# The norm of the next block from columns of the prompt, in blocks 1 to 3 of layer 0

## The chip, the cores and the metric

The kernel runs on one core of a Trainium2 chip. The metric is the time of one execution in microseconds of the device: a median of 2242.0 us in 3 runs (2238.49 to 2245.57). On the core, TensorE (PE) does matmuls and transposes, VectorE (DVE), ScalarE (ACT) and GpSimd (POOL) work on elements, and SyncE (SP) issues nearly all transfers from one queue, in program order.

## The reference

The reference is one step of a decoder with two layers, on a prompt of 2048 tokens and a batch of eight single new tokens. The width is 1024. Each layer normalises its input, projects it to 3332 columns, lets four token mixers (retention, HGRN2, S5, Mamba-2) work on groups of these columns, gates and joins their outputs, projects back and adds the result to the stream. The change touches the norm alone:

```
def rms_norm(x, w):
    xf = x.astype(jnp.float32)
    y = xf * lax.rsqrt(jnp.mean(xf * xf, axis=-1, keepdims=True) + EPS)
    return (y * w.astype(jnp.float32)).astype(x.dtype)
```

Every token is divided by the root mean square of its row, and every column is multiplied by a weight. The projections are computed in float32 precision from pairs of rounded values: each operand is split into a high part (fp32r) and a low part, the rest, and three matmuls (low by high, high by low, high by high) add up to one product.

## The kernel before

The prompt is cut into four blocks of 512 tokens, and each layer goes through its four blocks, so that there are eight blocks in all. For each block the normalised input stands in eight tiles hn, one for every 128 columns, each 128 columns (partitions) by 512 tokens, with a high and a low half. The matmuls want columns on the partitions, while the stream lies in memory by rows, a token after the other. So the norm has to transpose.

The projection of a block is made in four parts, gemm_A, gemm_H, gemm_M and gemm_S. The norm of the next block runs during the last, gemm_S: norm_stats has read the rows of the next block before that and has their reciprocal root mean squares in a small tile xn_rs (128 tokens by 4). norm_block (L567 to L596) is a generator of five steps, called between the passes of the last four pairs of gemm_S (L633 is the matmul of these passes). Its steps are:

- fetch (L570 to L577) brings 256 columns of all 512 rows into one of two xn buffers (L572, 512 KB). ACT multiplies two of the four groups of rows by xn_rs (L575, two instructions), and DVE the other two (L577, one instruction).
- For each of the two groups of 128 columns in a fetch, PE transposes four squares of 128x128 into a PSUM bank (L589), ACT writes the high half of hn from that bank times the weight (L591), and DVE writes the low half as the bank times the weight less the high half (L592).
- The next fetch into the same buffer follows.

PE runs in the order of the program. The other engines and their queues are ordered by a scheduler, which puts ready instructions by priority: weights (L687 to L689, load, cast and rest; L615 and L616 for the other kind of projection) have the highest, token mixers (L912 to L925 for HGRN2, L1604 to L1653 for Mamba-2, where one step of 128 tokens has its transposes L1604 and L1605, the matmuls L1611 and L1615, and later L1632, L1636 and L1639) come behind. Of the rest of what the prediction names: L793 adds up the four parts of the projection of the eight single tokens from a PSUM bank; L1585 is a multiplication on POOL; L502 to L526 are the setup of the S5 tables, with transfers through scratch tables in memory (s5c, gpad); L534 is the reading of rows by norm_stats. PSUM banks of the token mixers and the transposes come from one pool of four (mb), which go round in the order of the program. SG below is the second half of gemm_S, and RV the projection of the next part that follows it, whose matmul is L695; its weights go through six buffers wr.

Of the kernel before, what the change touches and what calls it, by code (L numbers as in the profile page):

```python
# [11 lines left out]
F32 = mybir.dt.float32  # L12
F32R = mybir.dt.float32r
BF16 = mybir.dt.bfloat16
I32 = mybir.dt.int32
AF = mybir.ActivationFunctionType
ALU = mybir.AluOpType
# [4 lines left out]
P = 128  # L22
D = 1024
KT = 8
TB = 512
# [88 lines left out]
def trunk_kernel(ctx: ExitStack, tc: tile.TileContext, A: dict):  # L114
    nc = tc.nc
    V, G, S, T = nc.vector, nc.gpsimd, nc.scalar, nc.tensor
# [12 lines left out]
    hnp = pool("hn", NHN)  # L129
    wrp = pool("wraw", NWR)  # L130
    whp = pool("whl", NWH)
    xnp = pool("xn", NXN)
# [13 lines left out]
    def nm(s):  # L146
        uid[0] += 1
        return f"{s}_{uid[0]}"
# [6 lines left out]
    def half(shape=(P, 512), dt=F32):  # L155
        if alt[0] and AH[alt[0]]:
            return smp.tile(list(shape), dt, name=nm("half"), tag="half" + alt[0], bufs=AH[alt[0]])
        return halfp.tile(list(shape), dt, name=nm("half"), tag="half")
# [22 lines left out]
    def mbank():  # L181
        return mps.tile([P, 512], F32, name=nm("mb"), tag="mb")
# [7 lines left out]
    mats = ctile([P, M_W], "mats")  # L190
    x_first = [big() for _ in range(4)]
    nw_rows = half([P, P])[0:8]
    with tc.high_priority(offset=2000):
        nc.sync.dma_start(x_first[0], x_in[0:P, :])
        nc.sync.dma_start(mats[:, 0:P], A["c_mats"][:, 0:P])
        nc.sync.dma_start(nw_rows, A["norm_w"][0].rearrange("(a p) -> a p", p=P))
        nc.sync.dma_start(x_first[1], x_in[P : 2 * P, :])
# [4 lines left out]
    lvl = ctile([P, 127], "lvl", I32)  # L202
    nc.sync.dma_start(lvl, A["c_lvl"])
    ident = mats[:, M_ID : M_ID + P]
# [335 lines left out]
    def norm_first(hn):  # L540
        ps = mbank()
        T.transpose(ps[:, 0:8], nw_rows, mats[:8, M_ID : M_ID + 8])
        nw = small([P, 8], "nw_first", bufs=1)
        V.tensor_copy(nw, ps[:, 0:8])
        rss = []
        for tt, xt in enumerate(x_first):
            ss, rs = small([P, 1], "nf_ss", bufs=4), small([P, 1], "nf_rs", bufs=4)
            S.activation(half((P, 1024), BF16), xt, AF.Square, accum_out=ss)
            rsqrt(rs, ss, 1, 1.0 / D)
            rss.append(rs)  # L550
        for tt, xt in enumerate(x_first):
            tsl = slice(tt * P, (tt + 1) * P)
            rs = rss[tt]
            V.tensor_scalar(xt, xt, rs, None, ALU.mult)
            for k4 in range(2):
                ps = mbank()
                for i in range(4):
                    kt = 4 * k4 + i
                    T.transpose(ps[:, i * P : (i + 1) * P], xt[:, kt * P : (kt + 1) * P], ident)
                for i in range(4):  # L560
                    kt = 4 * k4 + i
                    pk = ps[:, i * P : (i + 1) * P]
                    S.activation(hn[kt][:, 0, tsl], pk, AF.Identity, scale=nw[:, kt : kt + 1])
                    V.scalar_tensor_tensor(hn[kt][:, 1, tsl], pk, nw[:, kt : kt + 1], hn[kt][:, 0, tsl].bitcast(F32), ALU.mult, ALU.subtract)
            yield 0

    def norm_block(L, rows, rs, hn):  # L567
        xts = {}
# [1318 lines left out]
    layers = []  # L1887
    for l in range(DEPTH):
        L = Layer()
# [58 lines left out]
    with tc.manual_schedule(engines={mybir.EngineType.PE}):  # L1948
# [19 lines left out]
        for i, B in enumerate(blocks):  # L1968
            nxt = blocks[i + 1] if i + 1 < nblk else None
# [24 lines left out]
            rows, rs = norm_stats(nxt.b, srcdst(nxt.l)[0])  # L1994
# [9 lines left out]
                drain(prep)  # L2004
            if nxt.l != B.l:
                drain(load)
            norm = norm_block(layers[nxt.l], rows, rs, nxt.hn)
            run(gemm_S(B.L, B), lambda n: next(norm, 0) if n >= 3 else None)
            for _ in norm:
                pass  # L2010
# [42 lines left out]
```

## Time and profile before

| | before |
|---|---|
| median of 3 runs | 2242.0 us (2238.49 to 2245.57) |
| the profiled execution | 2245.02 us |
| its span | 2243.2 us |
| mean granted clock of PE | 0.98 |
| PE busy | 2118.9 us, 94% |
| DVE busy | 1669.3 us, 74% |
| ACT busy | 1034.2 us, 46% |
| POOL busy | 239.5 us, 11% |
| bytes moved | 284.41 MB, mean 127 GB/s |

The span is the stretch of the profiled execution from its first to its last instruction. Busy shares are means over the whole; the work in one stretch is read from views of that stretch alone. An engine with a full share there sets how fast the others get on.

### The profile page before, as it was taken

How to read it: one execution, taken by the hardware profiler on the slowest of the kernel's cores; microseconds unless marked ns; L12 is line 12 of the kernel's file. 1: busy time of each engine (PE TensorE's matmuls, PEld its weight loads, DVE VectorE, ACT ScalarE, POOL GpSimd, SP SyncE). 2: the span in 40 equal slices, each digit the busy share in tenths (PEclk: the TensorE clock that was granted, in tenths of full speed). 3: DMA queues.
4: the chain of work that ended last, by engine and by line, in shares of the span. 5: the costliest groups of instructions: out<-in, count | busy, mean ns of one | idle time of the engine just before them, and what ended most of it. 6: DMA issues, size and time to landing. Idle time of an engine off the chain costs nothing. (4 is left out here: it accounts for less than half of the span.)

```text
span 2243.2 us, 41062 instructions
## 1 busy us (share of the span) xinstructions
PE 2118.9 (94%) x15031; PEld 1712.8 (76%) x15031; DVE 1669.3 (74%) x4614; ACT 1034.2 (46%) x1889; POOL 239.5 (11%) x212
## 2 busy tenths in 40 slices
PE   7999989999999999999999998999899899999996
PEld 7778767776777877788877876777677678878786
DVE  6888666898749977787747867489985687748774
ACT  7434433456333564346453453444634245454343
POOL 0112011000210002201100011000120001100100
PEclk9999999999999999999999999999999999999999
DMA  6324633236524364374533335334652253431272
GB/s 213 104 66 120 182 104 118 90 108 203 143 67 143 94 196 121 115 167 126 179 97 112 95 113 165 99 109 119 202 154 78 86 163 101 156 92 50 68 260 94
DMA packets 263354, 284.41 MB, mean 127 GB/s; under 512 B 88752, under 2 KB 183616, under 8 KB 263152
## 3 DMA queue, kind: packets, MB, share of 16 engines
q1 hardware_dynamic: 263152, 281.79, 42.4%
q8 instruction: 118, 1.93, 0.4%
q14 instruction: 84, 0.69, 0.1%
HBM read 245.52 MB, written 31.99 MB: 124 GB/s over the span
## 5 line engine op out<-in xcount | busy, mean ns | idle before, releaser
L695 PE MATMUL gb<-wh,hn 128*128 128x512 f32 x2208 | 542.1, 400 | 3.4 <-DVE half L1650 2.3
L633 PE MATMUL gb<-hn,wh 128*128 128x512 f32 x1920 | 485.9, 406 | 10.3 <-DVE wh L616 6.9
L695 PEld LDWEIGHTS gb<-wh,hn 128*128 128x128 f32 x2208 | 409.9, 188 | 109.1 <-issue 11.6
L633 PEld LDWEIGHTS gb<-hn,wh 128*128 128x128 f32 x1920 | 359.9, 192 | 99.2 <-DVE wh L616 8.1
L689 DVE TENSOR_TENSOR wh<-wr,wh 128x512 fp32r<-128x512 f32 x296 | 215.3, 732 | 242.6 <-ACT wh L688 239.2
L688 ACT CAST wh<-wr 128x512 fp32r<-128x512 f32 x296 | 183.2, 620 | 373.5 <-PE gb L695 193.6
L695 PE MATMUL gb<-wh,mx 128*128 128x512 f32 x1344 | 341.5, 407 | 7.9 <-DVE half L1733 5.8
L695 PEld LDWEIGHTS gb<-wh,mx 128*128 128x128 f32 x1344 | 251.3, 192 | 77.8 <-DVE half L1733 10.1
L615 ACT CAST wh<-wr 128x512 fp32r<-128x512 f32 (+1 forms) x248 | 152.3, 619 | 308.4 <-PE gb L633 83.5
L616 DVE TENSOR_TENSOR wh<-wr,wh 128x512 fp32r<-128x512 f32 (+1 forms) x248 | 183.3, 745 | 77.6 <-ACT wh L615 74.2
L628 PE MATMUL gb<-wh,hn 128*128 128x256 f32 (+1 forms) x1728 | 220.2, 286 | 11.1 <-DVE convc L1524 4.7
L628 PEld LDWEIGHTS gb<-wh,hn 128*128 128x128 f32 x1728 | 211.6, 191 | 15.8 <-issue 9.2
L1585 POOL TENSOR_TENSOR half<-mats,m_lal 128x512 fp32r<-128x512 f32 x64 | 75.5, 1198 | 829.1 <-DVE m_lal L1579 278.8
L1330 DVE COPY_PREDICATED big<-lvl,mb 64x256 f32<-64x256 int32 x192 | 95.3, 537 | 2.5
L1297 ACT COPY zbH<-big 64x512 f32<-64x512 f32 x112 | 70.8, 632 | 48.5 <-PE mb L1306 35.9
L1523 DVE SCALAR_TENSOR_TENSOR big<-gb,vt,big 128x511 f32<-128x511 f32 (+2 forms) x96 | 71.1, 743 | 3.9 <-ACT big L1521 3.5
L1306 PE MATMUL mb<-zbH,big 128*64 128x64 f32 x1536 | 56.9, 229 | 11.0 <-DVE half L1177 5.3
L1306 PEld LDWEIGHTS mb<-zbH,big 128*64 128x64 f32 x1536 | 50.8, 142 | 20.5 <-issue 15.4
L1281 POOL TENSOR_TENSOR big<-mats,h_dg 128x1024 f32<-128x1024 f32 x16 | 30.7, 1942 | 241.8 <-DVE h_dg L1278 197.6
L1482 PE MATMUL mb<-big,big 128*64 128x128 f32 x512 | 40.6, 307 | 15.1 <-DMA big<-s5c 14.7
L628 PE MATMUL gb<-wh,mx 128*128 128x256 f32 x384 | 47.3, 282 | 4.7 <-DVE mx L1505 2.8
L1482 PEld LDWEIGHTS mb<-big,big 128*64 128x64 f32 x512 | 33.6, 155 | 23.7 <-issue 17.0
(497 smaller groups left out, 3091.2 us busy)
## 6 DMA issues: line engine op xcount, KB each, us to landing
wr<-in_w_in SPq DMA_DIRECT2D x416, 256.0 KB
wr<-in_w_out SPq DMA_DIRECT2D x128, 256.0 KB
big<-s5c SPq DMA_DIRECT2D x64, 256.0 KB
xn<-xmid SPq DMA_DIRECT2D x32, 512.0 KB
xn<-in_x_prompt SPq DMA_DIRECT2D x24, 512.0 KB
big<-s5c SPq DMA_DIRECT2D x24, 512.0 KB
xmid<-half SPq DMA_DIRECT2D x44, 256.0 KB
half<-xmid SPq DMA_DIRECT2D x44, 256.0 KB
```

The costliest lines, as they stand in the source:

```text
L615: S.copy(hl[:, 0, :, :n], raw[:, :, :n])
L616: V.tensor_tensor(hl[:, 1, :, :n], raw[:, :, :n], hl[:, 0, :, :n].bitcast(F32), ALU.subtract)
L628: T.matmul(o, lhs[2 * ks[ki] + k][:, a, tt * P : (tt + 1) * P], hls[ki][:, c, k, :n], start=(ki == 0 and k == 0 and pi == 0 and tt % per = ...
L633: T.matmul(banks[i], hls[ki][:, a, k, i * P : (i + 1) * P], lhs[2 * ks[ki] + k][:, c, :], start=(ki == 0 and k == 0 and pi == 0), stop=(ki ...
L688: S.copy(hl[:, 0, 0:512], raw[:, 0:512])
L689: V.tensor_tensor(hl[:, 1, 0:512], raw[:, 0:512], hl[:, 0, 0:512].bitcast(F32), ALU.subtract)
L695: T.matmul(banks[tt], lhs[ks[kt]][:, a, tt * P : (tt + 1) * P], hls[kt][:, c, 0:512], start=(kt == 0 and pi == 0), stop=(kt == KT - 1 and ...
L1306: T.matmul(ps[su, j * 64 : (j + 1) * 64], k[:, j // 4, (j % 4) * P + 64 * u : (j % 4) * P + 64 * u + 64], qz[:, :, j * 64 + 32 * u : j * 6 ...
L1330: V.copy_predicated(stv[p][su, :, nu * u : nu * u + nu, :], mv, ps[su, p * 256 : p * 256 + 256].rearrange("p (c b h) -> p c b h", c=8, h=h))
L1482: T.matmul(ps[64 * hb : 64 * hb + 64, g4 * P : (g4 + 1) * P], lhs, (tq if i else cq)[:, hb, g4], start=(i == 0), stop=(i == 1))
L1523: V.scalar_tensor_tensor(acc[:, 3 - i :], ps[:, : TB - 3 + i], w(i), acc[:, 3 - i :], ALU.mult, ALU.add)
L1585: E('m').tensor_tensor(mms[tt][i].rearrange("p (h t) -> p h t", h=4), tri[:, None, :].to_broadcast([P, 4, P]), lal[:, i, tt, :][:, :, None ...
```

## The change

For a next block of layer 0 a new generator norm_columns takes the place of norm_block. The host hands over the prompt a second time, transposed (c_xT, 1024 columns by 2048 tokens), and the fetches read two groups of 128 columns by 512 tokens from it, the same 512 KB, with no transpose. The factors xn_rs have to lie along the free axis then: PE transposes each of their four columns, broadcast to 128x128, into a bank, and ACT copies that bank to a half tile rb. DVE multiplies each fetched tile by rb (one instruction of 128x1024), and the high and low halves are written as before, by ACT and DVE, from the fetched tile and no longer from PSUM. A fetch into a buffer of xn follows the two subtractions that read it; before, it followed the transposes. The next block is in layer 0 for blocks 1, 2 and 3; for the other four norms that run within gemm_S the kernel is as it was. Line numbers below L192 are the same in both, those from L193 to L566 are one higher in the new kernel, and those from L567 on are 30 higher.

```diff
@@ -190,6 +190,7 @@
     mats = ctile([P, M_W], "mats")
     x_first = [big() for _ in range(4)]
     nw_rows = half([P, P])[0:8]
+    xT = A["c_xT"].rearrange("(k p) t -> p k t", p=P)
     with tc.high_priority(offset=2000):
         nc.sync.dma_start(x_first[0], x_in[0:P, :])
         nc.sync.dma_start(mats[:, 0:P], A["c_mats"][:, 0:P])
@@ -564,6 +565,35 @@
                     V.scalar_tensor_tensor(hn[kt][:, 1, tsl], pk, nw[:, kt : kt + 1], hn[kt][:, 0, tsl].bitcast(F32), ALU.mult, ALU.subtract)
             yield 0
 
+    def norm_columns(b, L, rs, hn):
+        xts = {}
+
+        def fetch(k2):
+            xt = xnp.tile([P, 2, TB], F32, name=nm("xn"), tag="xn")
+            nc.sync.dma_start(xt, xT[:, 2 * k2 : 2 * k2 + 2, b * TB : (b + 1) * TB])
+            xts[k2] = xt
+
+        fetch(0)
+        fetch(1)
+        ps = mbank()
+        for tt in range(4):
+            T.transpose(ps[:, tt * P : (tt + 1) * P], rs[:, tt : tt + 1].to_broadcast([P, P]), ident)
+        rb = half()
+        S.copy(rb, ps)
+        yield
+        for k2 in range(KT // 2):
+            xt = xts.pop(k2)
+            V.tensor_tensor(xt, xt, rb[:, None, :].to_broadcast([P, 2, TB]), ALU.mult)
+            for j in range(2):
+                kt = 2 * k2 + j
+                h = hnp.tile([P, 2, TB], F32R, name=nm("hn"), tag="hn")
+                S.activation(h[:, 0, :], xt[:, j], AF.Identity, scale=L.norm[:, kt : kt + 1])
+                V.scalar_tensor_tensor(h[:, 1, :], xt[:, j], L.norm[:, kt : kt + 1], h[:, 0, :].bitcast(F32), ALU.mult, ALU.subtract)
+                hn.append(h)
+            if k2 + 2 < KT // 2:
+                fetch(k2 + 2)
+            yield
+
     def norm_block(L, rows, rs, hn):
         xts = {}
 
@@ -2004,7 +2034,7 @@
                 drain(prep)
             if nxt.l != B.l:
                 drain(load)
-            norm = norm_block(layers[nxt.l], rows, rs, nxt.hn)
+            norm = norm_block(layers[nxt.l], rows, rs, nxt.hn) if nxt.l else norm_columns(nxt.b, layers[0], rs, nxt.hn)
             run(gemm_S(B.L, B), lambda n: next(norm, 0) if n >= 3 else None)
             for _ in norm:
                 pass
@@ -2037,7 +2067,7 @@
     rot, rotd, mats, lvl = shape_constants(seq)
     arrays, aps = {}, {}
     feed = {n: np.ascontiguousarray(inputs[n]) for n in _INS}
-    feed.update(c_rot=rot, c_rotd=rotd, c_mats=mats, c_lvl=lvl)
+    feed.update(c_rot=rot, c_rotd=rotd, c_mats=mats, c_lvl=lvl, c_xT=np.ascontiguousarray(inputs["x_prompt"][0].T))
     for name, a in feed.items():
         arrays[f"in_{name}"] = a
         aps[name] = nc.dram_tensor(f"in_{name}", a.shape, mybir.dt.from_np(a.dtype), kind="ExternalInput").ap()
```

PE, where the norm of block 1 begins, before (L589 is a transpose of the norm; L500 and L506 belong to the S5 setup):

```order
L633 MATMUL gb_2537<-hn_144,wh_2538 128x512 x3
L589 MATMUL mb_2555<-mats,xn_2504 128x128 x4
L589 MATMUL mb_2563<-mats,xn_2504 128x128 x4
L500 MATMUL mb_2577<-mats,big_2378 128x128 x4
L500 MATMUL mb_2585<-mats,big_2378 128x128 x4
L506 MATMUL mb_2592<-half_2371,big_2378 128x32 x8
L633 MATMUL gb_2536<-hn_145,wh_2624 128x512 x3
L633 MATMUL gb_2537<-hn_145,wh_2624 128x512 x3
L633 MATMUL gb_2536<-hn_146,wh_2624 128x512 x3
L633 MATMUL gb_2537<-hn_146,wh_2624 128x512 x3
L589 MATMUL mb_2641<-mats,xn_2509 128x128 x4
L589 MATMUL mb_2649<-mats,xn_2509 128x128 x4
```

And now (L580 is the transpose of xn_rs, L663 what was L633, L501 and L507 what was L500 and L506):

```order
L580 MATMUL mb_2508<-mats,xn_rs_1503 128x128 x4
L764 MATMUL mb_2515<-mats,half_1912 128x128 x2
L764 MATMUL mb_2515<-mats,half_2199 128x128 x2
L1621 MATMUL mb_2523<-m_la_2364,mats 128x16 x3
L663 MATMUL gb_2537<-hn_143,wh_2539 128x512 x3
L663 MATMUL gb_2538<-hn_143,wh_2539 128x512 x3
L663 MATMUL gb_2537<-hn_144,wh_2539 128x512 x3
L663 MATMUL gb_2538<-hn_144,wh_2539 128x512 x3
L501 MATMUL mb_2566<-mats,big_2378 128x128 x4
L501 MATMUL mb_2574<-mats,big_2378 128x128 x4
L507 MATMUL mb_2581<-half_2371,big_2378 128x32 x8
L663 MATMUL gb_2537<-hn_145,wh_2613 128x512 x3
```

The four transposes of the row of factors stand ahead of the passes, and between these no transposes of the norm are left: eight instructions went out at each of four places.

SP, in the middle of that block: the fetch for block 2 (L572), the loads of the S5 table (L525) and the weights of the next projection (L687), before:

```order
L534 DMA xn_4625<-in_x_prompt 128x1024
L526 DMA s5c_2_129<-big_2718 128x1024
L572 DMA xn_5425<-in_x_prompt 128x4x256
L572 DMA xn_5430<-in_x_prompt 128x4x256
L525 DMA big_2728<-gpad_1807 128x8x16 x8
L687 DMA wr_3088<-in_w_in 128x512
L687 DMA wr_3093<-in_w_in 128x512
L687 DMA wr_3150<-in_w_in 128x512
L687 DMA wr_3190<-in_w_in 128x512
```

And now (L573 is the fetch, L526 and L527 were L525 and L526, L717 was L687):

```order
L573 DMA xn_5384<-in_c_xT 128x2x512
L573 DMA xn_5386<-in_c_xT 128x2x512
L526 DMA big_2686<-gpad_1807 128x8x16 x2
L717 DMA wr_3047<-in_w_in 128x512
L717 DMA wr_3052<-in_w_in 128x512
L717 DMA wr_3109<-in_w_in 128x512
L717 DMA wr_3149<-in_w_in 128x512
L526 DMA big_2686<-gpad_1807 128x8x16 x6
L527 DMA s5c_2_129<-big_2686 128x1024
L526 DMA big_2696<-gpad_1807 128x8x16 x8
```

Four loads of weights stood behind all loads of the S5 table, and stand behind two of them now.

DVE, at the end of the norm of block 2, before (L793 is the sum of the single tokens' parts):

```order
L592 SCALAR_TENSOR_TENSOR hn_5601<-mb_5596,vt_428,hn_5601 128x512
L577 TENSOR_TENSOR xn_5551<-xn_5551,xn_rs_4628 128x512
L592 SCALAR_TENSOR_TENSOR hn_5609<-mb_5604,vt_428,hn_5609 128x512
L920 TENSOR_TENSOR big_5511<-big_5511,half_5326 128x1024
L689 TENSOR_TENSOR wh_5935<-wr_5936,wh_5935 128x512
L793 TENSOR_TENSOR half_5635<-half_5635,mb_5459 8x256
L592 SCALAR_TENSOR_TENSOR hn_5647<-mb_5642,vt_428,hn_5647 128x512
L793 TENSOR_TENSOR half_5635<-half_5635,mb_5459 8x256
L592 SCALAR_TENSOR_TENSOR hn_5655<-mb_5650,vt_428,hn_5655 128x512
L793 TENSOR_TENSOR half_5635<-half_5635,mb_5459 8x256
L1642 TENSOR_TENSOR hM_5672<-hM_5672,mb_5667 128x128
L1648 TENSOR_TENSOR half_5675<-mb_5658,m_ec_5439 128x256
```

And now (L586 is the multiplication of a fetched tile, L591 the low half, L823 what was L793, L719 what was L689):

```order
L719 TENSOR_TENSOR wh_5853<-wr_5854,wh_5853 128x512
L591 SCALAR_TENSOR_TENSOR hn_5533<-xn_5444,vt_428,hn_5533 128x512
L591 SCALAR_TENSOR_TENSOR hn_5536<-xn_5444,vt_428,hn_5536 128x512
L823 TENSOR_TENSOR half_5562<-half_5562,mb_5419 8x256
L586 TENSOR_TENSOR xn_5490<-xn_5490,half_5393 128x1024
L823 TENSOR_TENSOR half_5562<-half_5562,mb_5419 8x256
L1006 TENSOR_TENSOR half_5285<-half_5285 128x16
L1008 TENSOR_TENSOR half_5285<-half_5285 128x16
L823 TENSOR_TENSOR half_5562<-half_5562,mb_5419 8x256
L1007 TENSOR_TENSOR half_5285<-half_5285 128x16
L591 SCALAR_TENSOR_TENSOR hn_5570<-xn_5490,vt_428,hn_5570 128x512
L591 SCALAR_TENSOR_TENSOR hn_5573<-xn_5490,vt_428,hn_5573 128x512
```

The last two low halves stood ahead of the third of these sums and stand behind it now; the multiplication of the last fetch stands ahead of it, and L920 is no longer among these rows.

## Rows read from the trace of the kernel before

**Rows 1.** the page: its first line and the first line of part 1

```profile
span 2243.2 us, 41062 instructions
...
PE 2118.9 (94%) x15031; PEld 1712.8 (76%) x15031; DVE 1669.3 (74%) x4614; ACT 1034.2 (46%) x1889; POOL 239.5 (11%) x212
```

**Rows 2.** busy time in 20 us stretches: us, then busy (xcount) of each engine, clock, DMA

```profile
...
core 0: us, PE busy (x) PEld busy (x) DVE busy (x) ACT busy (x) POOL busy (x), PEclk, DMA share, GB/s
200.00:220.00 20.00, 20.00 (x131) 17.67 (x130) 19.52 (x40) 10.82 (x22) 10.11 (x7) 1.00 0.56 160
500.00:520.00 20.00, 16.67 (x115) 12.18 (x114) 19.38 (x38) 15.98 (x27) 3.04 (x3) 1.00 0.81 248
780.00:800.00 20.00, 17.54 (x107) 13.87 (x106) 19.88 (x56) 15.73 (x28) 3.94 (x4) 1.00 0.78 222
```

**Rows 3.** timeline of PE: start us, us, engine, line, operation, tiles, count, [idle before]

```profile
...
206.97 1.04 PE L589 MATMUL mb<-mats,xn 128*128 128x128 f32 x8
207.84 1.04 PE L500 MATMUL mb<-mats,big 128*128 128x128 f32 x8
```

**Rows 4.** one line of the kernel at a time, L592: durations in ns min/median/max

```profile
...
L592 DVE SCALAR_TENSOR_TENSOR hn<-mb,vt,hn x56: 733/743/752, 209.5 to 1896.8; 128x512 fp32r<-128x512 f32 x56
```

**Rows 5.** the same view, L577

```profile
...
L577 DVE TENSOR_TENSOR xn<-xn,xn_rs x28: 671/684/1505, 39.5 to 1890.0; 128x512 f32<-128x512 f32 x28
```

**Rows 6.** the same view, L575

```profile
...
L575 ACT ACTIVATE xn<-xn,xn_rs x56: 492/508/528, 39.5 to 1890.4; 128x256 f32<-128x256 f32 x56
```

**Rows 7.** groups by line and form, DVE, whole span: count, busy us, mean ns, idle before

```profile
...
L1246 DVE SCALAR_TENSOR_TENSOR big<-half,lbt,big 128x512 f32<-128x512 f32 x16 | 12.0, 748 | 0.6
...
L923 DVE TENSOR_TENSOR big<-big,half 128x1024 f32<-128x1024 f32 x6 | 8.1, 1357 | 0.0
...
L914 DVE TENSOR_TENSOR big<-half 128x1024 f32<-128x1024 f32 x6 | 7.3, 1219 | 0.1
```

**Rows 8.** timeline of PE, second transition

```profile
...
516.82 0.70 PE L1611 MATMUL mb<-half,strict_r 128*128 128x512 f32 x2 [2.35 <-DVE half L793]
```

**Rows 9.** timeline of DVE, the same moment

```profile
...
515.47 0.75 DVE L592 SCALAR_TENSOR_TENSOR hn<-mb,vt,hn 128x512 fp32r<-128x512 f32 x1
516.25 0.42 DVE L793 TENSOR_TENSOR half<-half,mb 8x256 f32<-8x256 f32 x1
```

**Rows 10.** what PE waited for from 760 to 830 us: total, times, longest

```profile
...
PE mb L589 <- DVE hn L592: 1.4, 1, 1.4
```

**Rows 11.** timeline of SP, its DMA issues from 232 to 250 us

```profile
...
233.86 2.44 SPq L572 DMA_DIRECT2D xn<-in_x_prompt  x2
236.43 8.59 SPq L525 DMA_DIRECT2D big<-gpad  x8
245.12 1.95 SPq L687 DMA_DIRECT2D wr<-in_w_in  x4
```

**Rows 12.** timeline of ACT from 240 to 250 us

```profile
...
248.24 0.62 ACT L688 CAST wh<-wr 128x512 fp32r<-128x512 f32 x1 [3.71 <-DMA wr<-in_w_in]
```

**Rows 13.** timeline of DVE from 248 to 254 us

```profile
...
251.85 0.69 DVE L689 TENSOR_TENSOR wh<-wr,wh 128x512 fp32r<-128x512 f32 x1 [0.71 <-ACT wh L688]
252.46 0.42 DVE L1621 TENSOR_TENSOR half<-half,m_dt 128x256 f32<-128x256 f32 x1
```

**Rows 14.** timeline of PE from 246 to 262 us

```profile
...
253.02 1.12 PE L1632 MATMUL mb<-half,half 128*64 128x64 f32 x16 [2.78 <-DVE half L1621]
```

**Rows 15.** three stretches behind waits of PE; the granted clock stands after POOL

```profile
...
253.00:257.00 4.00, 3.98 (x29) 3.38 (x30) 2.60 (x7) 0.00 (x0) 0.00 (x0) 0.57 0.00 0
301.00:308.00 7.00, 6.57 (x16) 5.17 (x17) 5.19 (x8) 3.26 (x6) 2.10 (x2) 0.52 0.27 77
516.00:520.00 4.00, 3.18 (x14) 2.43 (x15) 3.74 (x11) 3.26 (x5) 0.70 (x1) 1.00 0.74 213
```

**Rows 16.** timeline of PE from 300 to 303 us

```profile
...
301.43 2.08 PE L633 MATMUL gb<-hn,wh 128*128 128x512 f32 x4 [4.01 <-DVE wh L616]
```

**Rows 17.** timeline of POOL from 755 to 830 us

```profile
...
776.21 4.05 POOL L1585 TENSOR_TENSOR half<-mats,m_lal 128x512 fp32r<-128x512 f32 x4 [114.48 <-DMA s5c<-big]
```

## The prediction, made before the changed kernel ran

> **What bounds the kernel now.** I read the page first, then busy time in stretches of 20 us, and last the waits of PE and what stands around each in time. The page has PE busy for 2118.9 of 2243.2 us [rows 1], so over the whole span PE is the bound, and a transpose less should be worth its own time. The stretches tell more. At the three places where the changed norm runs (about 200 to 255, 485 to 545 and 764 to 820 us) DVE is busy for 19.52, 19.38 and 19.88 of 20 us, while PE has 20.00, 16.67 and 17.54 [rows 2]. In the second and third it is PE that waits there, and DVE that doesn't rest. The reader is to see this inversion: the change takes work from an engine that waits in those stretches and lays some on the one that is full. What PE waits for bears it out: 2.35 us for the third of the sums L793 on DVE, which ends at 516.67 us [rows 8, 9], and 1.4 us in the third stretch for L592 [rows 10].
>
> **The change part by part.**
>
> *PE.* In a block 32 transposes go (eight at each of four places) and four come. From the start of eight L589 at 206.97 to that of the next work at 207.84 it is 0.87 us [rows 3], 0.109 us each, so 28 fewer are 3.05 us a block and 9.1 us in three. That is what PE is spared, and the most that comes out of it where PE alone sets the pace. The four new transposes have a broadcast column as an operand, which no row shows; I take the same 0.109 us each. If each cost the start-to-start time of eight, 0.87 us, 3.0 us a block would be lost again; if nothing, 0.4 us would be gained.
>
> *DVE.* Four L577 of 684 ns go, 2.74 us. Four products of 128x1024 come. Nearest are L914 with 1219 ns and L923 with 1357 ns, a mean in which some run beside POOL [rows 5, 7]; with L914's, 4.88 us. The low halves read SBUF twice in place of PSUM and SBUF. L592 takes 743 ns [rows 4], and L1246, of the same size and form with all operands in SBUF, 748 [rows 7], so I count nothing. DVE gets 2.1 us more a block (2.7 with L923). Moreover the old L577 of the first two fetches are done long before the stretch; the new products aren't, as rb is made where the norm begins. Within the full stretch it is therefore 4 x 1.219 less 2 x 0.684, or 3.5 us.
>
> *ACT.* Eight L575 of 508 ns go [rows 6]; a copy of 128x512 comes, 0.62 us if it is like L688 [rows 12]. ACT is spared 3.4 us a block, and in the stretches it isn't the full engine [rows 2]; I count nothing. The high halves read SBUF and not PSUM; L688 does that in 0.62 us.
>
> *SP.* In block 1 the queue is reordered. Before, L525's eight transfers held SP from 236.43 for 8.59 us, and the four weights L687 went out at 245.12 [rows 11]. So ACT waited 3.71 us for one, DVE's L689 waited for ACT, L1621 stood behind L689 on DVE, and PE's L1632 waited 2.78 us for L1621 [rows 12 to 14]. Now the weights go out behind two L525, some six transfers of 1.07 us or 6.4 us sooner. Landing some 6 us earlier they take away more than the 2.78 us. And the wait cost twice: in the four microseconds behind it PE was granted 0.57 of its clock [rows 15], near the lower of its two levels, 0.43 x 4 = 1.7 us of work lost. Both together are 4.5 us. Should the buffers of the weights come free no sooner, it is nothing.
>
> *The fetches.* They move the same 512 KB. Each but the first two is issued only after both low halves of the buffer's last tile, where before it was issued after PE had transposed. So data come later by about two low halves and one product, 2.7 us, and in a stretch where DVE has other work to do this hides, mostly.
>
> *What of this reaches the end.* Block 1: PE runs ahead at first, but DVE is full until 220 us, and what Mamba-2's second L1632 needs of it stands behind products and low halves, so I take no gain up to there; then the 4.5 us. Block 2: before the third L793, 8 L592 and 2 L577 stood on DVE, 7.3 us of them; now 4 products and 6 low halves, 4.88 + 4.49 = 9.4 us, but L920, 1.2 us, and some short ones have gone behind. The third L793 thus ends within half a microsecond of where it did. PE comes there up to 3.05 us sooner and waits the longer. Behind it two low halves and L920 are late next, 1.5 and 1.2 us of DVE's; as some of it fits into PE's own work I take +1 us. Block 3: PE waits for L592 already, and what transposes it is spared goes into such waits; behind them the last two low halves are late by their own 1.5 us, of which some 0.5 were waited before. I take +1. For each block the ends are -3.05 (all of PE's time) and +3.5 us (all of DVE's).
>
> *The clock.* In block 2 PE's wait before L1611 would grow from 2.35 to some 4.5 us (2.35 and 3.05, less what it waits before). Behind the wait of 2.35 the clock stayed at 1.00, behind that of 2.78 it fell, and behind one of 4.01 us, L633's at 301.43, it was at 0.52 for 7 us, 3.4 us lost [rows 15, 16]. Whether it falls I give even chances, and the price is the mean of 1.7 and 3.4: half of 2.55, 1.3 us, in block 2. Sum: block 1 -4.5, block 2 +1.0 and +1.3, block 3 +1.0, together -1.2 us. From the profiled execution's 2245.0 us (1.8 of it outside the span, which the change doesn't touch) that is 2243.8; the execution lies 3.0 over the median of the runs, so against that it is 2240.8, about 2241.
>
> *A rule that speaks against the change.* A row first: L577, two tensors in SBUF, took 671 to 1505 ns with a median of 684, while L592, one in PSUM and one in SBUF, never took more than 752 in 56 [rows 4, 5]. The Trainium skill, "SBUF — State Buffer", section "SBUF: two separate sides", says that DVE and GpSimd share a pair of ports, held for a whole instruction, and that a DVE instruction with two SBUF inputs is among those that block. By that rule the 24 low halves, which read SBUF twice now, become open to POOL. The trace agrees for L577; for the new instructions nothing shows it yet.
>
> **The rivals.**
>
> *A: PE was the bound, and all of it comes out.* For it: 94% over the span, and PE busy for all of 200 to 220 us [rows 1, 2]. Against it: in the other two stretches PE waits for DVE already [rows 8, 10]. It gives 9.1 us and the 4.5 of the SP queue, 2242.0 - 13.6 = 2228; with the queue's part missing or half the transposes' coming through, 2233 to 2235.
>
> *B: DVE sets the pace at the three transitions, and it is slower.* The mechanism is the 3.5 us more that DVE has within each full stretch. It decides if the second L1632 of Mamba-2 waits for DVE in all three blocks. Then 3 x 3.5 = 10.5 us less the queue's 4.5, +6; with POOL in the way of three low halves of a block (1505 less 684 ns, 0.8 us each, by L577), 7 us more in three. POOL has a run of 4.05 us in block 3's stretch [rows 17]. It gives 2248 to 2255. Against it: the scheduler lays other DVE work behind these, and DVE has room again from 220 (block 1) and from 800 us.
>
> *C: nothing changes at all*, as the freed PE time is waited away and the SP queue's weights wait for free buffers: +0 to +2, 2242 to 2244.
>
> **How the numbers follow.** A change under 0.3%, some 6.7 us, cannot be told from none here. My forecast (2236 to 2245 by itself) has 0.45, C 0.12, A 0.25, B 0.18. Forecast and C lie within the bound but for their edges; A is faster but for its weakest form; B is slower but for its weakest. That makes faster 0.27, same 0.54, slower 0.19. For 8 in 10 the range takes in A with the queue's part or half of the transposes, and B's lower end: 2231 to 2250.
>
> **What would show it.** Right: PE busy some 9 us lower in sum and PE idle higher by about as much; no wait of L1632 near 250 us and no fall of the clock behind it; a longer wait of L1611 in block 2, with a fall of the clock behind it; DVE products near 1.22 us and low halves near 0.75. Wrong: DVE with idle time before the third L793 of block 2, which would say that PE's time came out (A); low halves of 1 us and more, and a second L1632 waiting for DVE by 3 us in every block (B); the weights L687 still landing near 248 us (no 4.5 us).

## The result, and the profile after

The changed kernel takes 2255.1 us (median of 6 runs, 2249.3 to 2260.4) against 2242.2 for the kernel before (6 runs, 2238.5 to 2245.6): a ratio of 1.006, with a 95% interval of 1.0041 to 1.0079. It is some 13 us slower, where 2241 was forecast and the range ended at 2250.

The head of the page after, its span and part 1, answers to [rows 1]:

```profile
span 2253.6 us, 40858 instructions
...
PE 2117.2 (94%) x14947; PEld 1710.4 (76%) x14947; DVE 1675.2 (74%) x4614; ACT 1027.7 (46%) x1868; POOL 241.1 (11%) x212
```

PE's busy time fell by 1.7 us and not by 9, and DVE's rose by 5.9, about three times the 2.1 counted for a block. Whole-span shares say no more than that. What says more is a stretch cut at marks of the work and not of time. I take each transition from PE's L1591 (after: L1621), a matmul of Mamba-2's at its beginning, to the start of the fourth and last L1632 (after: L1662). Before, by the view of busy time (columns as in [rows 2]):

```profile
...
204.00:253.02 49.02, 45.02 (x287) 36.12 (x287) 38.34 (x88) 26.55 (x52) 11.04 (x8) 1.00 0.76 186
491.34:542.27 50.93, 45.63 (x279) 34.29 (x278) 49.33 (x112) 33.01 (x62) 4.79 (x5) 1.00 0.68 213
775.23:819.65 44.42, 41.96 (x256) 33.38 (x255) 39.75 (x111) 28.32 (x52) 9.03 (x8) 1.00 0.63 182
```

And after, between the same two marks in blocks 1, 2 and 3:

```profile
...
207.72:256.66 48.94, 44.90 (x256) 34.88 (x255) 41.01 (x92) 25.83 (x48) 10.12 (x8) 0.93 0.57 150
492.44:547.23 54.79, 43.55 (x248) 31.90 (x247) 52.74 (x114) 31.78 (x59) 5.79 (x4) 0.91 0.62 197
784.06:833.53 49.47, 41.15 (x225) 32.45 (x224) 44.44 (x126) 26.42 (x48) 8.90 (x8) 0.93 0.59 164
```

The reader is to compare DVE's busy time with the length. In block 2 the stretch grew by 3.86 us (50.93 to 54.79) and DVE's work in it by 3.41; in block 3 by 5.05 (44.42 to 49.47) and 4.69. DVE's idle time in them stayed (1.6 and 2.1 us, 4.7 and 5.0). In block 1 DVE got 2.67 us more and the stretch is as long as it was: there DVE had 10.7 us of room, now 7.9. PE's idle time meanwhile grew from 5.3 to 11.2 us in block 2 and from 2.5 to 8.3 in block 3, and stayed at 4.0 in block 1. The three together are 8.8 us longer, of 10.4 that the span grew. By the same marks the rest are offsets, both ways, of this one pair of executions: the first stretch begins 3.7 us later, behind work that the change doesn't touch; 2.5 us are made up between the first and the second; 3.9 are lost between the second and the third (PE's waits for ACT's L1182 and for a table from memory are 3.6 us longer there); and 3.5 are made up behind the third.

The granted clock, the number after POOL, fell too: 1.00 in all three stretches before, 0.93, 0.91 and 0.93 after. PE went to the lower of its two levels in every block, behind waits of 1.44 and 2.45 us in block 1, within one of 8.68 in block 2, and at waits of 3.14 and 3.18 in block 3. In blocks 1 and 3:

```profile
...
216.00:218.00 2.00, 2.00 (x6) 1.52 (x6) 0.74 (x6) 0.72 (x1) 1.00 (x1) 0.50 0.88 263
233.00:236.00 3.00, 3.00 (x8) 2.32 (x9) 3.00 (x10) 1.82 (x5) 0.00 (x0) 0.50 0.78 288
803.00:805.00 2.00, 1.81 (x6) 1.57 (x7) 2.00 (x4) 2.00 (x5) 0.81 (x1) 0.50 0.60 222
817.00:819.00 2.00, 2.00 (x8) 1.72 (x7) 1.46 (x5) 1.26 (x2) 0.00 (x0) 0.50 0.71 271
```

PE's work lost to the clock can be added up as 1 less the granted clock, times PE's busy time, in windows of 1 us over the three transitions (200 to 264, 485 to 556 and 770 to 850 us). It is 8.8 us after and 1.7 before, where the clock fell once, behind the wait for L1632 [rows 15]. So PE's busy time hardly fell, though 84 transposes are gone. It is not this execution alone: the median of the mean granted clock is 0.973 in the 6 runs of the changed kernel, and 0.979 in 24 runs of the kernel before.

Where PE waited in block 2, its timeline, which answers to [rows 8]:

```profile
...
508.91 0.71 PE L1641 MATMUL mb<-half,strict_r 128*128 128x512 f32 x2
518.30 1.19 PE L1645 MATMUL mb<-zbM,big 128*128 128x256 f32 x2 [8.68 <-DVE half L1007]
...
520.03 2.93 PE L725 MATMUL gb<-wh,hn 128*128 128x512 f32 x6
...
531.43 0.70 PE L1645 MATMUL mb<-zbM,big 128*128 128x256 f32 x2 [1.59 <-DVE hM L1672]
```

And DVE at that moment, which answers to [rows 9]:

```profile
...
514.10 1.41 DVE L591 SCALAR_TENSOR_TENSOR hn<-xn,vt,hn 128x512 fp32r<-128x512 f32 x2
515.53 0.41 DVE L823 TENSOR_TENSOR half<-half,mb 8x256 f32<-8x256 f32 x1
515.88 1.21 DVE L586 TENSOR_TENSOR xn<-xn,half 128x1024 f32<-128x1024 f32 x1
517.11 0.42 DVE L823 TENSOR_TENSOR half<-half,mb 8x256 f32<-8x256 f32 x1
...
517.73 0.42 DVE L823 TENSOR_TENSOR half<-half,mb 8x256 f32<-8x256 f32 x1
...
518.17 1.40 DVE L591 SCALAR_TENSOR_TENSOR hn<-xn,vt,hn 128x512 fp32r<-128x512 f32 x2
```

PE came to the matmul that waits (L1645, that was L1615; before, it was L1611) at 509.6 and not at 514.5, five microseconds sooner, and waited 8.68 us in place of 2.35. The profile names L1007, which ended last; what PE's bank waits for is, as I read it, the third L823 at 517.73, the sum that was L793. It ended at 518.15 against 516.67, and the whole block had begun 1.1 us later. So up to here the forecast holds: the sum is late by less than half a microsecond, and all of PE's time is waited away. Behind it things went on to get worse, with the clock and with a wait of 1.59 us for the state L1672:

```profile
...
518.00:523.00 5.00, 4.66 (x10) 2.82 (x10) 4.97 (x13) 2.91 (x6) 1.37 (x1) 0.50 0.82 286
523.00:528.00 5.00, 4.86 (x34) 3.80 (x36) 4.08 (x9) 4.47 (x10) 0.65 (x1) 1.00 0.48 151
```

The granted clock stands after POOL: 0.50 for five microseconds, at the lower level, after the long wait. In block 3 there are three waits of over a microsecond where before there was one, of 1.4 us [rows 10], two of them for DVE and one for ACT, which itself had waited for a product:

```profile
...
798.51 0.69 PE L1662 MATMUL mb<-half,half 128*64 128x64 f32 x16 [1.31 <-DVE half L1649]
...
803.19 0.69 PE L1634 MATMUL mb<-mats,big 128*128 128x128 f32 x2 [3.14 <-ACT big L1426]
...
814.82 0.69 PE L1662 MATMUL mb<-half,half 128*64 128x64 f32 x16 [3.18 <-DVE half L1649]
```

### The profile page after: what moved, and what is told of

Its sections match the earlier page's. It is cut to its first block, busy times and chain, and to the rows that moved or that the text cites. A ratio compares the mean times of both kernels' runs of the same rounds, so it can differ in the third digit from the quotient of the medians.

```text
span 2253.6 us, 40858 instructions
## 1 busy us (share of the span) xinstructions
PE 2117.2 (94%) x14947; PEld 1710.4 (76%) x14947; DVE 1675.2 (74%) x4614; ACT 1027.7 (46%) x1868; POOL 241.1 (11%) x212
## 5 line engine op out<-in xcount | busy, mean ns | idle before, releaser
L663 PE MATMUL gb<-hn,wh 128*128 128x512 f32 x1920 | 487.0, 407 | 9.9 <-DVE wh L646 7.4
L663 PEld LDWEIGHTS gb<-hn,wh 128*128 128x128 f32 x1920 | 362.1, 193 | 99.1 <-DVE wh L646 8.4
L719 DVE TENSOR_TENSOR wh<-wr,wh 128x512 fp32r<-128x512 f32 x296 | 218.9, 744 | 233.1 <-ACT wh L718 228.3
L1615 POOL TENSOR_TENSOR half<-mats,m_lal 128x512 fp32r<-128x512 f32 x64 | 77.0, 1223 | 814.8 <-DVE m_lal L1609 167.3
L1512 PE MATMUL mb<-big,big 128*64 128x128 f32 x512 | 37.7, 293 | 16.3 <-DMA big<-s5c 16.1
L1163 POOL TENSOR_TENSOR half<-half,half 128x256 f32<-128x256 f32 x32 | 32.4, 1014 | 178.5 <-DVE half L1161 163.4
```

The lines of the kernel that those rows point to most:

```text
L663: T.matmul(banks[i], hls[ki][:, a, k, i * P : (i + 1) * P], lhs[2 * ks[ki] + k][:, c, :], start=(ki == 0 and k == 0 and pi == 0), stop=(ki ...
L719: V.tensor_tensor(hl[:, 1, 0:512], raw[:, 0:512], hl[:, 0, 0:512].bitcast(F32), ALU.subtract)
L1615: E('m').tensor_tensor(mms[tt][i].rearrange("p (h t) -> p h t", h=4), tri[:, None, :].to_broadcast([P, 4, P]), lal[:, i, tt, :][:, :, None ...
```

## The experiments

Two theories stood against each other. Theory Q: DVE's queue is the bound in the transitions, and what DVE got there sets the loss. Theory K: PE's spared time gathers in one long wait, and the clock that falls behind it sets the loss. Later a third came in, theory O: any change makes the scheduler lay DVE's instructions in another order, and another order can be the worse one, whatever the amount of work. Each ratio is to the kernel before, run beside it on the same chip; each row of a trace is from one profiled execution.

**No product.** The four products of a block are left out, and so the rows are not scaled.

```diff
-            V.tensor_tensor(xt, xt, rb[:, None, :].to_broadcast([P, 2, TB]), ALU.mult)
```

> The changed kernel with its four products of a fetched tile by the row of factors left out in each of blocks 1 to 3 (the rows are not scaled then), so 4.9 us less of DVE a block; PE is as in the changed kernel. Theory Q (the work that DVE got in the stretches where it is full decides): DVE has 2.7 us a block less than even before, the long wait of PE in block 2 shrinks below 5 us, and the time is about 2236, under before. Theory K (what decides is that PE's spared time gathers in one long wait, behind which its clock falls; DVE's work is the lesser part): PE still runs ahead of DVE, waits and loses clock; 2245 to 2250.

Measured: 2242.8 us, ratio 1.0001 (0.9984 to 1.0018), neither Q's number nor in K's range. All of the loss is gone with the products. But it is no faster than before, though PE and DVE both have less to do. Block 2's stretch, the second row, shows why:

```profile
...
206.71:255.88 49.17, 43.44 (x255) 33.67 (x255) 37.77 (x86) 25.89 (x48) 10.27 (x8) 0.97 0.66 165
489.99:547.16 57.17, 48.85 (x247) 36.43 (x246) 49.90 (x113) 32.00 (x60) 6.29 (x6) 0.82 0.54 173
781.85:824.14 42.29, 39.87 (x224) 31.16 (x223) 37.21 (x95) 25.83 (x46) 9.57 (x8) 0.96 0.65 182
```

Block 3 is 2.1 us shorter than before, and block 2 is 6.2 longer at a granted clock of 0.82, with DVE's work the same (49.90 against 49.33). Two waits of PE, 2.5 and 2.8 us, stand close together there. In the three transitions PE lost 11.9 us of work to the clock, 8.6 of them in block 2. So what theory K describes is there in this stretch, and it is large enough to eat what the spared work gives. It doesn't make the kernel slower than before.

**Idle transposes.** The changed kernel with 32 transposes a block back on PE, unused.

```diff
+                ps = mbank()
+                for tt in range(4):
+                    T.transpose(ps[:, tt * P : (tt + 1) * P], xt[:, j, tt * P : (tt + 1) * P], ident)
                 h = hnp.tile([P, 2, TB], F32R, name=nm("hn"), tag="hn")
```

> The changed kernel with the 32 transposes a block put back on PE at their old places, on the fetched tile, their result unused; DVE, ACT and the transfers have the changed kernel's work, PE has 3.5 us a block more than that, and the PSUM banks go round as before. Theory K: the long wait is split up again, the clock falls less, and the time comes back to 2243 to 2247. Theory Q: DVE is as late as in the changed kernel, PE only waits less; 2253 to 2258, with waits shorter by what the transposes take.

Measured: 2258.5 us, ratio 1.0067 (1.0047 to 1.0087). The time did not come back, as K would have it. The trace kept of it is its fastest run, 2249.8 us, and so shows less than the median loss. In it the longest wait of PE in block 2 is 3.9 us in place of 8.7:

```profile
...
511.21 1.94 PE L591 MATMUL mb<-mats,xn 128*128 128x128 f32 x8 [3.90 <-DVE half L1008]
```

The wait is split up, yet PE lost 8.1 us of work to the clock in the three transitions, about as much as the 8.8 of the changed kernel. K falls as the main cause: with nothing spared on PE the loss stays, and the clock falls behind waits for DVE all the same.

**Products added to the kernel before.** One product on DVE behind each fetch's transposes, in layer 0.

```diff
                 hn.append(h)
+            if L.l == 0:
+                V.tensor_tensor(xt, xt, xt, ALU.mult)
             if k2 + 2 < KT // 2:
```

> The kernel before, with one more product of 128x1024 on DVE behind each fetch's transposes in blocks 1 to 3 (on data that are not used any more, ahead of the next fetch into that buffer): 4.9 us of DVE a block and a later fetch, with the transposes still on PE. Theory Q: as slow as the changed kernel or slower, 2252 to 2260. Theory K: PE has nothing spared that could gather, and waits for DVE in parts; 2244 to 2248.

Measured: 2260.6 us, ratio 1.0075 (1.0047 to 1.0103), as Q has it. No transpose was taken away, and the loss is there. In its transitions PE lost 7.9 us of work to the clock, so that fall comes with DVE's added work and needs no spared transposes.

**No product, with transposes.** Both edits at once, the fourth corner.

> The changed kernel without its products (rows not scaled) and with the 32 transposes a block back on PE, unused. Beside the same without the transposes (2242.8) it prices PE's spared time when DVE is not in the way. If the spared time is simply waited away, the same within 2 us. If it comes out, 6 to 10 us slower. If it does harm, as it gathers in long waits behind which the clock falls (theory K as a smaller term), 3 to 6 us faster.

Measured: 2248.2 us, ratio 1.0023 (1.0007 to 1.0039). The four corners by their medians:

| | no transposes | 32 idle transposes a block |
|---|---|---|
| no product | 2242.8 | 2248.2 |
| with products | 2255.1 (the changed kernel) | 2258.5 |

The products cost 12.3 and 10.3 us of the 14.6 that 12 by 1.213 make, and by the ratios both are clear of the intervals, which reach some 4 us to either side of each corner. The transposes cost 5.4 and 3.4 of the 10.5 us that 96 by 0.109 make, which is not clear of them. So DVE's time comes out in good part, nearly all of it by the medians; PE's is worth less by the medians, and the runs don't tell it from nothing.

**Two products early.** The row of factors and the first two products are made during gemm_M.

```diff
+        def product(k2):
+            V.tensor_tensor(xts[k2], xts[k2], rb[:, None, :].to_broadcast([P, 2, TB]), ALU.mult)
+        product(0)
+        product(1)
         yield
         for k2 in range(KT // 2):
+            if k2 > 1:
+                product(k2)
             xt = xts.pop(k2)
...
-            run(gemm_M(B.L, B))
+            run(gemm_M(B.L, B), lambda n: next(norm) if n == 8 and nxt.l == 0 else None)
```

> The changed kernel with the row of factors and the products of the first two fetches made earlier, during the projection ahead of gemm_S, where DVE has some room; two of the four products a block leave the full stretch, as two of the four multiplications of before did. Theory Q: about half of the loss comes back, 2246 to 2250. Theory K: PE is as far ahead as in the changed kernel, and DVE's chain ends 2.4 us sooner, so the wait is shorter but long; 2249 to 2254.

Measured: 2246.5 us, ratio 1.0018 (0.9997 to 1.0039). With two of four products out of the stretch, 8.6 of 12.9 us came back, more than half; Q's number holds at its low end. In its trace the three stretches are 1.4 us shorter in sum than before (142.9 against 144.4), though DVE has 4.6 us more work in them: it waits less there (10.9 us against 17.0). So the place of the work counts beside its amount. PE came to the transition of block 2 5.5 us ahead of the kernel before (at 477.99 against 483.51) and was 0.6 ahead at the start of the stretch; waits for DVE, of 1.3 and 2.8 us, stand between.

**Two early, and the sums first.** The sums at the end of a half get the priority of weights.

```diff
-                dec[1](n, dbank)
+                with tc.high_priority(offset=WPRI):
+                    dec[1](n, dbank)
```

> The version with two early products, and the sums of the single tokens' parts at the end of gemm_S given the priority of weights on ACT and DVE. In that version's trace PE waits 6.3 us for the third of these sums in block 2. If the place of this one sum behind the norm's work on DVE is what holds PE there (theory Q in its narrow form), the wait falls below 3 us and the time to 2240 to 2243; if DVE's whole load holds it, the next instruction of Mamba-2 waits as long and it stays at 2246 to 2248.

Measured: 2245.2 us, ratio 1.0002 (0.9985 to 1.0019), in neither range. Against the version before it the medians differ by 1.3 us, which the intervals don't tell apart. PE's waits in block 2 of the version with two early products, and of this one:

```profile
...
PE mb L1648 <- DVE half L830: 6.3, 1, 6.3
```

```profile
...
PE mb L1649 <- DVE half L831: 4.2, 1, 4.2
PE mb L1670 <- DVE rs L233: 3.0, 1, 3.0
```

The wait for the sum fell from 6.3 to 4.2 us, and one for another result of DVE's (L232 in that version), 24 us behind it, grew from 0.8 to 3.0. One instruction's place moves the wait; the two together stay at 7 us.

**Product made twice.** With the line of the product doubled the rows are scaled twice.

> The changed kernel with each product made twice (the rows are scaled twice then): 4.9 us a block more of DVE's time at the same place. If DVE's amount of work in the full stretch decides, the step from no product (2242.8) to one (2255.1) comes again: 2265 to 2270. If it was the new order, made once, that cost, the second product costs little: 2253 to 2259.

Measured: 2270.2 us, ratio 1.0126 (1.0096 to 1.0155). This is the point that speaks most for Q against O. No product, one and two: 2242.8, 2255.1, 2270.2, steps of 12.3 and 15.1 us for 14.6 us of DVE each. Its stretches:

```profile
...
206.30:259.60 53.30, 45.43 (x255) 34.87 (x254) 47.93 (x95) 25.61 (x48) 12.58 (x8) 0.90 0.55 139
497.60:558.99 61.39, 46.08 (x248) 34.31 (x247) 58.89 (x121) 33.53 (x61) 7.49 (x6) 0.83 0.58 178
793.93:846.52 52.59, 41.49 (x225) 33.20 (x224) 47.69 (x130) 27.11 (x48) 12.31 (x8) 0.90 0.54 155
```

They are 167.3 us long in sum against 153.2 with one product: 14.1 more, with 16.3 of DVE.

**Three buffers.** The changed kernel and the kernel before, each with NXN = 3; in the changed one fetches go out three ahead.

> The changed kernel with three buffers for fetched tiles and fetches issued three ahead, the products where they were. If the late fetch (each waits for the low halves of the tile before) is what costs, 2243 to 2248. If DVE's load is (theory Q), it stays at 2252 to 2258.

> The kernel before with three buffers for fetched tiles and nothing else: the control for the third buffer. If the third buffer by itself costs nothing, 2241 to 2245, and the 10 us by which three early products were slower than two have another cause; if its memory or the order of transfers that comes with it costs, 2250 or more.

Measured: 2253.4 us, ratio 1.0044 (1.0028 to 1.0060), and 2260.5, ratio 1.0066 (1.0048 to 1.0085). The control did what it was for: the third buffer alone makes the kernel before 17 us slower. Its second stretch:

```profile
...
494.71:551.28 56.57, 49.58 (x279) 37.58 (x278) 50.61 (x115) 33.26 (x61) 6.52 (x6) 0.91 0.62 193
```

DVE has 50.61 us of work in 56.57, so 6.0 us of idle time, where before it had 1.6. This is theory O, and it exists: the same work in another order, with DVE waiting. The traces show one place of it. The xn buffers also hold the rows that norm_stats reads; with the third one ACT works on such rows (L535) ahead of L1396, waits for their transfer, and PE waits 2.96 us for L1396, where it waited 0.61 before:

```profile
...
517.85 1.06 ACT L535 ACTIVATE xn<-xn 128x1024 f32<-128x1024 f32 x1 [2.49 <-DMA xn<-in_x_prompt]
```

```profile
...
521.45 1.12 PE L1632 MATMUL mb<-half,half 128*64 128x64 f32 x16 [2.96 <-ACT big L1396]
```

In the changed kernel DVE doesn't wait more in these stretches, so O alone does not account for its loss. But with three buffers the change costs nothing: 2253.4 against 2260.5, with intervals that overlap. The price of the products is thus that in the order of two buffers, and Q does not say what another order makes of them. Whether a late fetch costs something in the changed kernel can't be told from the pair, as with three buffers it is the faster of the two.

**Three products early, with three buffers.**

> The version with early products, with three buffers for the fetched tiles in place of two and three of the four products made early. Theory Q: 1.2 us of DVE a block leave the full stretch and the last fetch comes sooner: 2242 to 2245 against 2246.5 with two. If what two early products brought was the early fetch and no longer DVE's time, there is no change: 2246 to 2248.

Measured: 2256.8 us, ratio 1.0056 (1.0038 to 1.0074), a miss: 10 us slower than with two. The third buffer, which costs the kernel before 17 us, may be why. But it cost the changed kernel nothing (2253.4 against 2255.1), and beside that three early products brought nothing, which Q doesn't explain.

**Block 1 alone**, first as in the change, then with two early products.

```diff
-... if nxt.l else norm_columns(nxt.b, layers[0], rs, nxt.hn)
+... if nxt.l or nxt.b > 1 else norm_columns(nxt.b, layers[0], rs, nxt.hn)
```

> The norm from columns for block 1 alone; blocks 2 and 3 as before. By the trace of the changed kernel block 1 costs nothing in the end and blocks 2 and 3 cost 8 and 7 us: then 2239 to 2243. The prediction's step for block 1 (4.5 us gained by the reordered SP queue) would give 2238 to 2239. If each block costs a third of the whole loss, 2247.

> The version with two early products for block 1 alone, blocks 2 and 3 as in the kernel before. In the trace of the version for all three, block 1 ended 6.4 us ahead of the kernel before, and blocks 2 and 3 lost more than that. If those are separate, 2235 to 2239, faster than both kernels; if block 1's lead is waited away in block 2, 2241 to 2244.

Measured: 2243.7 us, ratio 1.0002 (0.9985 to 1.0020), and 2241.6, ratio 0.9990 (0.9973 to 1.0008). As in the change, block 1 costs nothing and gives nothing that can be seen, and the 4.5 us of the prediction, a ratio of 0.998, lie outside the interval. With early products its stretch is 4.7 us shorter:

```profile
...
207.97:252.31 44.34, 41.71 (x255) 32.71 (x255) 41.52 (x88) 25.74 (x48) 11.82 (x9) 1.00 0.63 159
```

It is 44.34 us against 49.02. But in this execution it began 4.0 us later than in the kernel before (207.97 against 204.00), behind work that the edit doesn't touch, so it ended only 0.7 us sooner, and what becomes of a lead can't be followed in it. This was the version with the best chance of beating both kernels; it can't be told from the kernel before, and a gain of 4.7 us lies within its interval too.

**The kernel before with all scaling on ACT** (NACT = 4).

> The kernel before with the rows of all four groups of a fetch scaled by ACT and none by DVE, in all norms of both layers: DVE has 2.74 us a block less, 1.4 of it in the full stretch, ACT 4.1 more, the transposes stay. Theory Q: a DVE microsecond in the stretch is worth about 0.8, so 2235 to 2240. If ACT, at 80 to 89% in the second stretch, becomes the bound, 2243 to 2250.

Measured: 2255.2 us, ratio 1.0049 (1.0033 to 1.0065), slower than either theory said. Relieving DVE did not help, and Q has no answer for it. In the trace kept of it, its slowest run, DVE has 4.8 us less in the three stretches, and they are 9.1 us longer. ACT isn't full (34.8 of 57.5 us in block 2), but its L791, on which the first of the sums L793 builds, stands behind the added L575, and PE's wait for L1611 there is 3.7 us in place of 2.35. That would make it the place of ACT's work ahead of the same sum; no run tests it, and it stays open.

**The last two products on POOL**, on top of two early ones.

```diff
-                product(k2)
+                G.tensor_tensor(xts[k2], xts[k2], rb[:, None, :].to_broadcast([P, 2, TB]), ALU.mult)
```

> The version with two early products, the other two made on POOL in place of DVE: 2.4 us a block of DVE's time less in the full stretch, POOL 3 to 4 us more. If DVE's amount decides and POOL is not in its way, 2241 to 2244 (against 2246.5). If POOL's two SBUF inputs hold DVE's instructions up, as L577 with 1505 ns and others beside POOL suggest, what is gained is lost again: 2246 to 2252.

Measured: 2257.7 us, ratio 1.0069 (1.0047 to 1.0092), 11 us slower than with them on DVE. POOL's product (L592 there) and DVE's low half (L598 there), by line, with count, busy us and mean ns:

```profile
...
L592 POOL TENSOR_TENSOR xn<-xn,half 128x1024 f32<-128x1024 f32 x6 | 16.2, 2700 | 26.3 <-DVE hn L598 9.6 <-DVE half L1688 8.4 <-DMA xn<-in_c_xT 8.3
```

```profile
...
L598 DVE SCALAR_TENSOR_TENSOR hn<-xn,vt,hn 128x512 fp32r<-128x512 f32 x24 | 23.2, 986 | 3.0 <-ACT hn L597 3.0
```

And one small DVE instruction, of 0.28 us elsewhere, beside POOL's product from 507.87 to 511.21:

```profile
...
508.98 2.37 DVE L1678 TENSOR_TENSOR hM<-hM,m_et 128x128 f32<-128x128 f32 x1
```

The product takes POOL 2.70 us, and DVE's low halves 986 ns in the mean where they were 740; the median is 744 and the longest 2856, so a few were held for long. Work taken off DVE and laid on POOL came back as longer instructions of DVE's: its busy time is 1680.9 us, with the products on it 1675.0.

## Why the prediction was wrong, step by step

The step that failed is "What of this reaches the end": block 1 -4.5, block 2 +1.0, block 3 +1.0 us, and 1.3 for the clock. The sum was made as if most of DVE's added work would go where DVE or PE had room. Measured, the three stretches are -0.1, +3.9 and +5.0 us, with 2.7, 3.4 and 4.7 us more of DVE's work in them, and the clock fell in all three. In blocks 2 and 3, where DVE was busy for 97 and 89% of the stretch, what was laid on it came out in full; in block 1, where it had 10.7 us of room, it did not. Over the whole kernel the products cost 12.3 us for 14.6 of DVE's, and 15.1 for the next 14.6. That was rival B, 3 x 3.5 us and more, to which 0.18 was given. Its mechanism on DVE is what the runs show, in two blocks of three. That its 2255 meets the number is luck in part: it has 7 us for POOL, which did not come, and takes off 4.5 for the SP queue, which did not come either. Both the 3.5 us and the full stretch stood in the text, and I let a walk through single waits overrule them. The walk was right for the third L793 in block 2, and wrong in the +1 us behind it: L920 and the last two low halves, which had gone behind that sum, were still to be done, and PE waited for DVE again there.

*DVE's terms* were right in size: the product took 1.213 us (1.219 counted) and the low half from SBUF 740 ns (748 counted). By line, with count, busy us and mean ns:

```profile
...
L591 DVE SCALAR_TENSOR_TENSOR hn<-xn,vt,hn 128x512 fp32r<-128x512 f32 x24 | 16.9, 740 | 1.3 <-ACT hn L590 1.3
...
L586 DVE TENSOR_TENSOR xn<-xn,half 128x1024 f32<-128x1024 f32 x12 | 14.5, 1213 | 0.3 <-DMA xn<-in_c_xT 0.3
```

*PE's term* was right in that it is waited away in block 2. Its size over the whole kernel stays open: the medians give 5.4 and 3.4 us for 10.5 us of transposes, which the runs don't tell from nothing.

*The SP queue.* The term of 4.5 us for block 1 failed in its mechanism. The wait for L1632 near 250 us is gone, and the clock behind it stayed at 1.00, as forecast. But the four weights went out at 248.07 us, three later than before and not six sooner. Ahead of them SP waited 8.2 us for a low half on DVE before it could read the next rows (L535, that was L534, into a buffer that the norm had held), where before it waited 1.9 for transposes; this is the late fetch that the prediction let hide. And a wait of 2.45 us came 20 us ahead of the old one, for L1680, which on DVE stands behind the norm's low halves. SP's wait, SP's issue of the weights, and PE:

```profile
...
SPq L535 <- DVE hn L591: 8.2, 1, 8.2
```

```profile
...
248.07 1.98 SPq L717 DMA_DIRECT2D wr<-in_w_in  x4
```

```profile
...
232.86 5.94 PE L725 MATMUL gb<-wh,hn 128*128 128x512 f32 x18 [2.45 <-DVE half L1680]
```

Behind the new waits the clock fell twice, and PE lost 3.3 us of work there, where 1.7 were to be gained. The block's stretch is as long as it was, and the version with this block alone has a ratio of 1.0002: nothing gained, where 4.5 us were counted.

*The clock* fell in block 2, which had been given even chances, behind 8.68 us of waiting and not 4.5, and cost 2.5 us there (0.50 for five microseconds), between the two prices. But it fell in blocks 1 and 3 too, which the sum did not have: 1.3 us less 1.7 were counted for it in all, and it took 8.8 less 1.7 of PE's work. How much of these 7 us reaches the end can't be separated from the waits, as both come together; without products more was lost, 11.9 us, and the kernel was as fast as before. As a cause apart from DVE's work it is ruled out by the idle transposes and by the products added to the kernel before.

*The rule of the Trainium skill on the shared ports* ("SBUF — State Buffer", section "SBUF: two separate sides") did not show in the changed kernel: its 24 low halves took 740 ns in the mean and at most 752; POOL's L1615 overlapped one of them, for 0.07 us. Where products were laid on POOL the trace agrees, for some of DVE's instructions beside them.

## What to carry to other kernels

Cut the profile at marks of the work and ask of each stretch which engine has idle time that would take the new work. If none has, the stretch grows by what is added, and the engine that was relieved waits, whatever its share of the whole span is. Idle time in the stretch need not be at the right place: in block 3 DVE had 4.7 us of it, and 4.7 us of added work came out all the same. It doesn't hold the other way round: with less work on DVE (no product, scaling on ACT) no version was faster than the kernel before. And read the granted clock of each stretch beside the busy times.

## What the runs showed of the hardware

Beside a POOL product with two SBUF inputs a DVE instruction of 128x128 took 2.37 us in place of 0.28, and the POOL product itself 2.70 us. Scaling on ACT from SBUF took no less time than from PSUM: the high half of 128x512 took 720 ns in the mean from SBUF (after, by line, count, busy us, mean ns) and 682 from PSUM (before):

```profile
...
L590 ACT ACTIVATE hn<-xn,vt 128x512 fp32r<-128x512 f32 x24 | 16.4, 720 | 24.2 <-DVE xn L586 22.2 <-PE gb L663 1.9
```

```profile
...
L591 ACT ACTIVATE hn<-mb,vt 128x512 fp32r<-128x512 f32 x56 | 35.4, 682 | 6.9 <-PE mb L589 6.9
```

Waits of PE of nearly the same length had a fall of the granted clock behind them or none: before the change it stayed at 1.00 behind 2.35 us [rows 8, 15], and after it PE was at 0.50 behind 2.45 us in block 1. The times of one kernel on one chip lie 10 to 20 us apart (2228 to 2249 in 24 runs of the kernel before, with a mean granted clock of 0.986 in the fastest and 0.977 in the slowest), so that a change of 3 us is not seen in a few runs, and the last steps above, of 1 to 3 us, were not resolved.
